# Seven-product blocks of a two-layer decoder trunk: the next block's weight split in eleven pieces, and another place for the sums of results

## The chip, the cores and the metric

The kernel runs on one core of one Trainium2 chip. The metric is the device time of one execution in microseconds (us). Engines are named as the profile names them: PE (TensorE, matmuls; PEld its weight loads), DVE (VectorE), ACT (ScalarE), POOL (GpSimd), SP (SyncE, which here only issues loads).

## The reference

The input is x, 512 tokens of 1024 channels, float32. Two layers of three sub-layers each, and a final norm:

```
for layer in (0, 1):
    x = x + 0.5 * swiglu(rmsnorm(x), w_gate, w_up, w_down)     # ffn1, inner width 2752
    x = x + mixer(rmsnorm(x))                                  # layer 0: S5 and attention; layer 1: short convolution
    x = x + 0.5 * swiglu(rmsnorm(x), w_gate, w_up, w_down)     # ffn2
out = rmsnorm(x)

def swiglu(h, w_gate, w_up, w_down):
    return (silu(h @ w_gate) * (h @ w_up)) @ w_down
```

The change touches the swiglu of layer 0's ffn2 and layer 1's ffn1 (n = 1 and n = 2 in the kernel, `SEVEN`).

## The kernel before, in words

**Precision.** Each float32 operand is split into a high part (a cast to a shorter float, on ACT, L214 for weights) and the rest (a subtraction on DVE, L220). A product of two operands is three matmuls: high by high, low by high, high by low. Weights arrive in a `raw` tile of 128 x 1024 (three of them), loaded by SP (L202); `refill` issues the load that reuses a raw tile once its last reader is done.

**Units.** A unit is one 128-row block of weights. `drive` runs a hand-written list of steps in order; every engine has one queue and works through it in that order. Ahead of a unit's matmuls `advance` splits the unit two places further on. The work of `ffn` comes in three thirds of the inner width. Each third first makes h (gate and up for its blocks f), then eight down units (dt = 0 to 7) that add to x, one per 128 channels. The down results use two PSUM banks (`ps_mm`), gate and up six (`ps_A`). After a down unit DVE adds the result to x (L539).

**Seven-product blocks.** For n = 1 and 2 the second and third third (seven blocks f each, 28 in all) are made with seven products of half size instead of eight (Winograd's form of Strassen's scheme). The weights of a block are the gate's halves A11, A12 and the up's halves A21, A22 along the channels; x is cut into halves B11, B12, B21, B22 along channels (first index) and tokens. With S1 = A21 + A22, S2 = S1 - A11, S3 = A11 - A21, S4 = A12 - S2 and T1 = B12 - B11, T2 = B22 - T1, T3 = B22 - B12, T4 = B21 - T2, one block issues on PE, all from line L667, 12 matmuls of 256 columns per product:

| | bank | product | what then reads the bank |
|---|---|---|---|
| 1 | x | A11 B11 | p1 = copy of x, ACT L687 |
| 2 | y | S2 T2 | u1 = y + p1, DVE L692 |
| 3 | x (added) | A12 B21 | silu, ACT L695: left half of the gate |
| 4 | y (added) | S1 T1 | u3 = y + p1, DVE L699 |
| 5 | z | S3 T3 | up_r = z + u3, DVE L703 |
| 6 | y (added) | S4 B22 | s_r = y + p1, DVE L706, then silu, ACT L707 |
| 7 | z (added) | A22 T4 | up_l = z + u1, DVE L709 |

After it h = s * up (DVE L710), its high part (ACT L713) and its low part (DVE L715). The low part is left in `pending` and runs in the next block or in `flush`. A product that adds to a bank must wait until the bank's reader is done: the third for p1, the fourth for u1, the sixth for u3, the seventh for up_r.

**The split of the next block** is handed out between the products by `more()`, which takes the next step of the generator `cuts`: first the gate's cast and subtraction (L214, L220), then `cut_mate` in four steps: cast of A22 (L262) with S1 (L263); S2 (L265) with the cast of S1, S2 (L266); S3 (L268), S4 (L269) and their cast (L270); the low part of A22 (L272) with two refills; then the two low parts of S (L278). `more()` is called right after a product's matmuls, ahead of the reader of its bank: after product 1 the gate's split stands ahead of p1, after product 2 the cast of A22 and S1 ahead of u1.

**Parts of x.** T1 to T4 and the parts of B are made once per ffn for four channel pairs i, in steps between the down units of the first third: `seven_sums(i)` (four DVE sums L627 to L632, four ACT casts L628 to L634) and `seven_lower(i)` (four DVE subtractions L642 to L646). `seven_parts(dt)` says which run after unit dt: sums 0 after dt 0, sums 1 and lower 0 after dt 1, lower 1 after dt 2, sums 2 after dt 3, lower 2 after dt 4, sums 3 after dt 5, lower 3 after dt 6. The split of the first seven-product block stands ahead of dt 6 and 7.

**The tail.** The inner width 2752 is 21 blocks of 128 and one of 64 + 64 (`TAIL`), whose h is made by a longer chain (L504 to L514). For n = 1 and 2 it is a unit of the first third, after f = 1; there the norm's factors become known, and two blocks' sums run late.

Of the kernel before, what the change touches and what calls it, by code (L numbers as in the profile page):

```python
# [8 lines left out]
F32 = mybir.dt.float32  # L9
# [3 lines left out]
ALU = mybir.AluOpType  # L13
# [8 lines left out]
TAIL = 21  # L22
# [121 lines left out]
class Trunk:  # L144
# [101 lines left out]

    def cut_mate(self, n):

        nc, sp = self.nc, self.sp7
        v = nc.vector
        u = self.units[n]
        g, w = u.mate.raw, u.raw
        a, b = slice(0, 512), slice(512, 1024)
        u.q_hi = sp.tile([128, 512], F32R, tag="ahi", name="ahi", bufs=2)
        u.q_lo = sp.tile([128, 512], F32R, tag="alo", name="alo", bufs=2)
        s = [sp.tile([128, 1024], F32, tag="s12", name="s12"), sp.tile([128, 1024], F32, tag="s34", name="s34")]
        u.s_hi = [sp.tile([128, 1024], F32R, tag="shi", name="shi", bufs=3) for _ in range(2)]  # L260
        u.s_lo = [sp.tile([128, 1024], F32R, tag="slo", name="slo", bufs=3) for _ in range(2)]
        nc.scalar.copy(u.q_hi, w[:, b])  # L262
        v.tensor_tensor(s[0][:, a], w[:, a], w[:, b], ALU.add)  # L263
        yield
        v.tensor_tensor(s[0][:, b], s[0][:, a], g[:, a], ALU.subtract)  # L265
        nc.scalar.copy(u.s_hi[0], s[0])  # L266
        yield
        v.tensor_tensor(s[1][:, a], g[:, a], w[:, a], ALU.subtract)  # L268
        v.tensor_tensor(s[1][:, b], g[:, b], s[0][:, b], ALU.subtract)  # L269
        nc.scalar.copy(u.s_hi[1], s[1])  # L270
        yield
        v.tensor_tensor(u.q_lo, w[:, b], u.q_hi.bitcast(F32), ALU.subtract)  # L272
        self.split = n + 1
        self.refill(n - 1)
        self.refill(n)
        yield
        for i in range(2):
            v.tensor_tensor(u.s_lo[i], s[i], u.s_hi[i].bitcast(F32), ALU.subtract)  # L278
            yield

    def drive(self):

# [175 lines left out]
    def ffn(self, n, nxt):  # L458
# [4 lines left out]
        nc = self.nc  # L463

        thirds = THIRDS[n]
# [82 lines left out]
        for third in range(3):  # L548
            seven = n in SEVEN and third
            if seven:  # L550
                pairs = [(Unit(gu[n, 2 * f], 1024, None, None), Unit(gu[n, 2 * f + 1], 1024, None, None)) for f in thirds[third]]
                for f, (g, u) in zip(thirds[third], pairs):
                    g.paired, u.mate = True, g
                    st.steps += [[g, u], lambda f=f, u=u: st.seven_products(f, u)]
                st.steps.append(st.flush)
            for f in [] if seven else sorted(thirds[third], key=lambda f: (f != TAIL or third == 0, f if f != TAIL else 1.5)):
                keep = []
                if f == TAIL:
                    st.steps.append(Unit(gu[n, 2 * f], 1024, st.over_x("A", keep), evac_tail(keep)))
                    continue  # L560
                g, u = evac_gate(keep, f), evac_up(keep, f)
                if f == 0:
                    early, keep0 = [g, u], keep
                    g = u = None
                    if n == st.first_ffn:
                        g, u = (lambda r=r: [st.feed_sq(st.first_norm, k) for k in r] for r in (range(4), range(4, 8)))
                elif f == 1:
                    def ug(g=g, u=u, keep=keep):
                        st.norm_bcast()
                        for kp, (gg, uu) in ((keep0, early), (keep, (g, u))):  # L570
                            pu = kp.pop()
                            gg()
                            kp.append(pu)
                            uu()
                    g, u = st.norm_sums, ug
                pair = [Unit(gu[n, 2 * f], 1024, st.over_x("A", keep), g), Unit(gu[n, 2 * f + 1], 1024, st.over_x("A", keep), u)]
                if f == 0 and n == st.first_ffn:
                    pair[0].products = lambda u, p=pair, k=keep: st.over_x_two("A", p, [k, k])
                    pair[1].products = lambda u: None
                st.steps += pair  # L580
                if n in SEVEN and 3 <= f < 7:
                    st.steps.append(lambda i=f - 3: st.seven_x(n, i))
            if third == 2 and nxt == 6:
                st.steps.insert(-1, st.advance)
                st.steps.append(st.advance)
                st.last_down([down(dt, third) for dt in range(NK)])
                break
            for dt in range(NK):
                s = down(dt, third)
                more = n in SEVEN and third < 2  # L590
                if more and dt == 6:
                    st.steps.append(st.advance)
                s.split_before = more and dt == 7
                st.steps.append(s)
                if more and third == 0:
                    st.steps += [lambda p=p: p() for p in st.seven_parts(dt)]
# [14 lines left out]

    def seven_parts(self, dt):

        i = {0: 0, 1: 1, 3: 2, 5: 3}.get(dt)
        j = {1: 0, 2: 1, 4: 2, 6: 3}.get(dt)
        return [lambda: self.seven_sums(i)] * (i is not None) + [lambda: self.seven_lower(j)] * (j is not None)

    def seven_sums(self, i):

# [27 lines left out]
        self.t7[i], self.b7[i] = (hi, lo), (b, o)  # L647

    def flush(self):
        if self.pending is not None:  # L650
            self.pending()
        self.pending = None

    def seven_products(self, f, u):

        nc, v, g = self.nc, self.nc.vector, u.mate
        cut = self.cuts(2)
        more = lambda: next(cut, None)
        l, r = slice(0, 256), slice(256, 512)

        def product(ps, w, c, b, first):

            for k in range(4):
                hi, lo = (p[:, c + k * 128:c + k * 128 + 128] for p in w)
                xhi, xlo = b(k)
                for n, (a, m) in enumerate(((hi, xhi), (lo, xhi), (hi, xlo))):
                    nc.tensor.matmul(  # L667
                        ps, a, m, start=first and k == 0 and n == 0, stop=k == 3 and n == 2, skip_group_check=True)

        def part(j):  # L670
            return lambda k: [p[:, j * 256:j * 256 + 256] for p in self.b7[k]]

        def total(j):
            c = slice(j % 2 * 256, j % 2 * 256 + 256)
            return lambda k: [p[j // 2][:, c] for p in self.t7[k]]

        b11, b21, b22 = (part(j) for j in range(3))
        t1, t2, t3, t4 = (total(j) for j in range(4))
        gate, s12, s34 = (g.hi, g.lo), (u.s_hi[0], u.s_lo[0]), (u.s_hi[1], u.s_lo[1])
        s = self.fp.tile([128, S], F32, tag="s", name="s", bufs=2)  # L680
        up = self.fp.tile([128, S], F32, tag="t", name="up", bufs=2)
        p1, u3 = up[:, l], s[:, r]
        u1 = self.tp.tile([128, S], F32, tag="sq", name="u1", bufs=2)[:, l]
        x = self.bank("A")[:, l]
        product(x, gate, 0, b11, True)
        more()
        nc.scalar.copy(p1, x)  # L687
        self.flush()
        y = self.bank("A")[:, l]
        product(y, s12, 512, t2, True)  # L690
        more()
        v.tensor_tensor(u1, y, p1, ALU.add)  # L692
        product(x, gate, 512, b21, False)
        more()
        nc.scalar.activation(s[:, l], x, AF.Silu)  # L695
        more()
        product(y, s12, 0, t1, False)
        more()
        v.tensor_tensor(u3, y, p1, ALU.add)  # L699
        z = self.bank("A")[:, l]  # L700
        product(z, s34, 0, t3, True)
        more()
        v.tensor_tensor(up[:, r], z, u3, ALU.add)  # L703
        product(y, s34, 512, b22, False)
        more()
        v.tensor_tensor(s[:, r], y, p1, ALU.add)  # L706
        nc.scalar.activation(s[:, r], s[:, r], AF.Silu)  # L707
        product(z, (u.q_hi, u.q_lo), 0, t4, False)
        v.tensor_tensor(up[:, l], z, u1, ALU.add)  # L709
        v.tensor_tensor(s, s, up, ALU.mult)  # L710
        hi = self.fp.tile([128, S], F32R, tag="hhi", name="hhi", bufs=8)
        lo = self.fp.tile([128, S], F32R, tag="hlo", name="hlo", bufs=8)
        nc.scalar.copy(hi, s)  # L713
        self.h[f] = (hi, lo)
        self.pending = lambda: v.tensor_tensor(lo, s, hi.bitcast(F32), ALU.subtract)  # L715
        deque(cut, maxlen=0)

    def last_down(self, units):
# [1218 lines left out]
```

## Time and profile before

| | |
|---|---|
| median of 3 runs (lowest to highest) | 1884.87 us (1883.11 to 1886.81) |
| profiled execution, its own time | 1882.82 us |
| its span, first to last instruction | 1881.1 us |
| busy in the span: PE, DVE, ACT, POOL | 97%, 64%, 37%, 6% |
| granted TensorE clock, mean | 0.996 of full speed |

The span is what the profile divides into shares; the rest of the profiled time lies around it. A busy PE is not a PE at its peak, since matmuls overlap and their ends are modelled: from one matmul's start to the next is the pace. In timeline rows the first number is the start in us from the span's start, the second the duration; [a <-b] is the engine's idle time before it and what ended it.

### The profile page before, as it was taken

The page shows a single profiled execution, that of the slowest core. Times are in us where ns is not written, and L with a number is a line of the kernel's source. Part 1 is how long each engine was busy: PE and PEld are TensorE (multiplying, and loading weights), DVE is VectorE, ACT ScalarE, POOL GpSimd, SP SyncE. Part 2 cuts the span into 40 slices and gives each one's busy share as a digit, 9 for nine tenths or more (in the row PEclk, how much of TensorE's full clock was granted, in tenths as well). Part 3 has the DMA queues.
Part 4 walks back from the last instruction along what each step waited for, and adds up shares of the span by engine and source line. Part 5 has one row for each costly group of instructions (what it writes and reads, how often), then busy time and mean ns, then how long its engine had stood idle before and what let it go on. Part 6 is the DMA issues. An engine that isn't in the chain of part 4 may idle for free.

```text
span 1881.1 us, 24317 instructions
## 1 busy us (share of the span) xinstructions
PE 1828.1 (97%) x9494; PEld 1558.1 (83%) x9494; DVE 1204.3 (64%) x1941; ACT 697.9 (37%) x1037; POOL 115.5 (6%) x238
## 2 busy tenths in 40 slices
PE   9999999999989999999999999999999999999998
PEld 8878888888867788888888888888888888888888
DVE  6757778656886568848756688576655545344444
ACT  5322322444885334424343344243322333222233
POOL 0280000100002000000010000000200110000000
PEclk9999999999989999999999999999999999999999
DMA  4334444456312232232232322322323223323331
GB/s 168 108 96 146 127 143 126 136 188 221 100 34 73 85 98 99 89 102 90 83 108 90 101 90 87 104 90 83 101 98 101 92 87 112 96 95 90 101 103 65
DMA packets 80146, 197.88 MB, mean 105 GB/s; under 512 B 20560, under 2 KB 29792, under 8 KB 80032
## 3 DMA queue, kind: packets, MB, share of 16 engines
q1 hardware_dynamic: 79856, 196.30, 32.5%
q8 instruction: 74, 1.21, 0.3%
q14 instruction: 40, 0.33, 0.1%
q10 hardware_dynamic: 144, 0.03, 0.0%
q0 software_dynamic: 32, 0.01, 0.0%
HBM read 180.45 MB, written 12.58 MB: 103 GB/s over the span
## 4 chain that ended last, share of the span: by engine, by line
PE 80%; DVE 8%; ACT 5%; issue 3%; POOL 3%; DMA 0%; DVEq 0%; SPq 0%; POOLq 0%; ACTq 0%
PE ps_A L302 13%; PE ps_A L301 13%; PE ps_A L303 13%; PE ps_A L667 10%; PE ps_mm L301 7%; PE ps_mm L302 7%; PE ps_mm L303 7%; ACT whi L214 2%; DVE wlo L220 1%; DVE s L710 1%; DVE hlo L715 1%; ACT hhi L713 1%; DVE s L263 1%; PE ps_mm L1640 1%; PE ps_A L1235 1%
## 5 line engine op out<-in xcount | busy, mean ns | idle before, releaser
L220 DVE TENSOR_TENSOR wlo<-raw,whi 128x1024 fp32r<-128x1024 f32 (+1 forms) x296 | 363.9, 1230 | 164.5 <-ACT whi L214 163.6
L302 PE MATMUL ps_A<-xhi,wlo 128*128 128x512 f32 x1120 | 436.4, 390 | 3.0 <-DVE wlo L220 2.9
L301 PE MATMUL ps_A<-xhi,whi 128*128 128x512 f32 x1120 | 437.6, 391 | 0.1
L303 PE MATMUL ps_A<-xlo,whi 128*128 128x512 f32 x1120 | 436.0, 389 | 0.1
L214 ACT CAST whi<-raw 128x1024 fp32r<-128x1024 f32 (+1 forms) x296 | 302.5, 1023 | 304.7 <-PE ps_mm L303 156.4
L301 PE MATMUL ps_mm<-hhi,whi 128*128 128x512 f32 (+1 forms) x672 | 256.7, 382 | 0.0
L302 PE MATMUL ps_mm<-hhi,wlo 128*128 128x512 f32 (+1 forms) x672 | 256.4, 382 | 0.0
L303 PE MATMUL ps_mm<-hlo,whi 128*128 128x512 f32 (+1 forms) x672 | 256.3, 381 | 0.0
L302 PEld LDWEIGHTS ps_A<-xhi,wlo 128*128 128x128 f32 x1120 | 210.3, 188 | 47.8 <-DVE wlo L220 4.4
L301 PEld LDWEIGHTS ps_A<-xhi,whi 128*128 128x128 f32 x1120 | 210.2, 188 | 45.4 <-ACT whi L214 0.9
L303 PEld LDWEIGHTS ps_A<-xlo,whi 128*128 128x128 f32 x1120 | 210.2, 188 | 44.3 <-DVE xlo L359 0.5
L301 PEld LDWEIGHTS ps_mm<-hhi,whi 128*128 128x128 f32 x672 | 126.3, 188 | 24.6 <-issue 0.4
L303 PEld LDWEIGHTS ps_mm<-hlo,whi 128*128 128x128 f32 x672 | 126.3, 188 | 24.4
L302 PEld LDWEIGHTS ps_mm<-hhi,wlo 128*128 128x128 f32 x672 | 126.3, 188 | 24.1
L539 DVE SCALAR_TENSOR_TENSOR x<-ps_mm,x 128x512 f32<-128x512 f32 x88 | 60.7, 690 | 108.1 <-PE ps_mm L303 100.7
L667 PE MATMUL ps_A<-thi,shi 128*128 128x256 f32 x336 | 97.7, 291 | 21.3 <-DVE u L692 21.3
L483 ACT ACTIVATE s<-t 128x512 f32<-128x512 f32 x56 | 35.4, 632 | 181.4 <-DVE t L481 181.4
L494 ACT CAST hhi<-s 128x512 fp32r<-128x512 f32 x56 | 34.8, 621 | 180.4 <-DVE s L493 180.4
L667 PE MATMUL ps_A<-thi,slo 128*128 128x256 f32 x336 | 95.0, 283 | 0.0
L667 PE MATMUL ps_A<-tlo,shi 128*128 128x256 f32 x336 | 95.0, 283 | 0.0
L667 PEld LDWEIGHTS ps_A<-thi,shi 128*128 128x128 f32 x336 | 64.3, 191 | 26.6 <-DVE u L692 26.6
L349 POOL TENSOR_TENSOR acc<-acc,sq 128x512 f32<-128x512 f32 x28 | 36.3, 1295 | 798.1 <-ACT sq L342 798.1
(404 smaller groups left out, 2940.6 us busy)
## 6 DMA issues: line engine op xcount, KB each, us to landing
raw<-gu SPq DMA_DIRECT2D x170, 512.0 KB, 3.4
raw<-dn SPq DMA_DIRECT2D x80, 448.0 KB, 3.3
raw<-sci SPq DMA_DIRECT2D x24, 512.0 KB, 3.4
raw<-dn SPq DMA_DIRECT2D x16, 512.0 KB, 3.5
raw<-ab SPq DMA_DIRECT2D x16, 512.0 KB, 3.5
raw<-abo SPq DMA_DIRECT2D x8, 512.0 KB, 3.5
raw<-sco SPq DMA_DIRECT2D x8, 512.0 KB, 3.4
x<-xT SPq DMA_DIRECT2D x8, 256.0 KB, 5.2
```

The source lines that it names most:

```text
L214: self.nc.scalar.copy(u.hi[:, : u.cols], u.raw[:, : u.cols])
L220: (engine or self.nc.vector).tensor_tensor(u.lo[:, :c], u.raw[:, :c], u.hi[:, :c].bitcast(F32), ALU.subtract)
L263: v.tensor_tensor(s[0][:, a], w[:, a], w[:, b], ALU.add)
L301: nc.tensor.matmul(ps, whi, xhi, start=start and i == 0, stop=False)
L302: nc.tensor.matmul(ps, wlo, xhi, start=False, stop=False)
L303: nc.tensor.matmul(ps, whi, xlo, start=False, stop=stop and i == n - 1)
L349: e.tensor_tensor(self.acc, self.acc, sq, ALU.add)
L483: nc.scalar.activation(s, t, AF.Silu)
L494: nc.scalar.copy(hi, s)
L539: nc.vector.scalar_tensor_tensor(x, keep[0], 0.5, x, ALU.mult, ALU.add)
L667: nc.tensor.matmul(ps, a, m, start=first and k == 0 and n == 0, stop=k == 3 and n == 2, skip_group_check=True)
L710: v.tensor_tensor(s, s, up, ALU.mult)
```

## The change

`cut_mate` becomes `mate_pieces`, which returns eleven named pieces; the last low part (of S3, S4) is cut in two. In a block whose follower is a seven-product block, `more(names)` issues pieces by name, and each reader of a bank stands right after the product that ends it, ahead of the pieces. After product 7 nothing is issued: up_l, the product with up, h's high part and its low part become a list in `pending`; the first three run after the next block's first product, ahead of p1, the low part behind the first pieces. `flush` runs all four at the end of a third. Where the follower is a down unit, its split is issued at two fixed places. `seven_parts` is: sums 0 and 1 after dt 0; lower 0, sums 2 after dt 1; lower 1, sums 3 after dt 2; lower 2 after dt 3; lower 3 after dt 4. The tail's unit moves from after f = 1 to after f = 4 (the sort key 1.5 becomes 4.5).

```diff
--- before.py
+++ after.py
@@ -246,6 +246,13 @@
     def cut_mate(self, n):
+        p = self.mate_pieces(n)
+        for i in ("a_hi", "s1", "s2", "s12_hi", "s3", "s4", "s34_hi", "a_lo", "s12_lo", "s34_lo0", "s34_lo1"):
+            p[i]()
+        yield
+    def mate_pieces(self, n):
@@ -259,24 +266,29 @@
         s = [sp.tile([128, 1024], F32, tag="s12", name="s12"), sp.tile([128, 1024], F32, tag="s34", name="s34")]
         u.s_hi = [sp.tile([128, 1024], F32R, tag="shi", name="shi", bufs=3) for _ in range(2)]
         u.s_lo = [sp.tile([128, 1024], F32R, tag="slo", name="slo", bufs=3) for _ in range(2)]
-        nc.scalar.copy(u.q_hi, w[:, b])
-        v.tensor_tensor(s[0][:, a], w[:, a], w[:, b], ALU.add)
-        yield
-        v.tensor_tensor(s[0][:, b], s[0][:, a], g[:, a], ALU.subtract)
-        nc.scalar.copy(u.s_hi[0], s[0])
-        yield
-        v.tensor_tensor(s[1][:, a], g[:, a], w[:, a], ALU.subtract)
-        v.tensor_tensor(s[1][:, b], g[:, b], s[0][:, b], ALU.subtract)
-        nc.scalar.copy(u.s_hi[1], s[1])
-        yield
-        v.tensor_tensor(u.q_lo, w[:, b], u.q_hi.bitcast(F32), ALU.subtract)
-        self.split = n + 1
-        self.refill(n - 1)
-        self.refill(n)
-        yield
-        for i in range(2):
-            v.tensor_tensor(u.s_lo[i], s[i], u.s_hi[i].bitcast(F32), ALU.subtract)
-            yield
+        def lower(i, c=slice(0, 1024)):
+            v.tensor_tensor(u.s_lo[i][:, c], s[i][:, c], u.s_hi[i][:, c].bitcast(F32), ALU.subtract)
+        def a_lo():
+            v.tensor_tensor(u.q_lo, w[:, b], u.q_hi.bitcast(F32), ALU.subtract)
+            self.split = n + 1
+            self.refill(n - 1)
+            self.refill(n)
+        return {
+            "a_hi": lambda: nc.scalar.copy(u.q_hi, w[:, b]),
+            "s1": lambda: v.tensor_tensor(s[0][:, a], w[:, a], w[:, b], ALU.add),
+            "s2": lambda: v.tensor_tensor(s[0][:, b], s[0][:, a], g[:, a], ALU.subtract),
+            "s12_hi": lambda: nc.scalar.copy(u.s_hi[0], s[0]),
+            "s3": lambda: v.tensor_tensor(s[1][:, a], g[:, a], w[:, a], ALU.subtract),
+            "s4": lambda: v.tensor_tensor(s[1][:, b], g[:, b], s[0][:, b], ALU.subtract),
+            "s34_hi": lambda: nc.scalar.copy(u.s_hi[1], s[1]),
+            "a_lo": a_lo,
+            "s12_lo": lambda: lower(0),
+            "s34_lo0": lambda: lower(1, a),
+            "s34_lo1": lambda: lower(1, b),
+        }
     def drive(self):
@@ -553,7 +565,7 @@
                     g.paired, u.mate = True, g
                     st.steps += [[g, u], lambda f=f, u=u: st.seven_products(f, u)]
                 st.steps.append(st.flush)
-            for f in [] if seven else sorted(thirds[third], key=lambda f: (f != TAIL or third == 0, f if f != TAIL else 1.5)):
+            for f in [] if seven else sorted(thirds[third], key=lambda f: (f != TAIL or third == 0, f if f != TAIL else 4.5)):
                 keep = []
                 if f == TAIL:
                     st.steps.append(Unit(gu[n, 2 * f], 1024, st.over_x("A", keep), evac_tail(keep)))
@@ -611,9 +623,8 @@
     def seven_parts(self, dt):
-        i = {0: 0, 1: 1, 3: 2, 5: 3}.get(dt)
-        j = {1: 0, 2: 1, 4: 2, 6: 3}.get(dt)
-        return [lambda: self.seven_sums(i)] * (i is not None) + [lambda: self.seven_lower(j)] * (j is not None)
+        return [lambda: self.seven_lower(dt - 1)] * (1 <= dt <= 4) + [
+            lambda i=i: self.seven_sums(i) for i in {0: (0, 1), 1: (2,), 2: (3,)}.get(dt, ())]
     def seven_sums(self, i):
@@ -647,15 +658,23 @@
         self.t7[i], self.b7[i] = (hi, lo), (b, o)
     def flush(self):
-        if self.pending is not None:
-            self.pending()
+        for p in self.pending or ():
+            p()
         self.pending = None
     def seven_products(self, f, u):
         nc, v, g = self.nc, self.nc.vector, u.mate
-        cut = self.cuts(2)
-        more = lambda: next(cut, None)
+        n = self.split
+        more = lambda *names: None
+        if n < len(self.units) and self.units[n].paired:
+            mate = self.mate_pieces(n + 1)
+            mate["hi"] = lambda: self.cut_hi(n)
+            mate["lo"] = lambda: self.cut_lo(n)
+            more = lambda *names: [mate[i]() for i in names]
+            cut = iter(())
+        else:
+            cut = self.cuts(2)
         l, r = slice(0, 256), slice(256, 512)
         def product(ps, w, c, b, first):
@@ -683,36 +702,43 @@
         u1 = self.tp.tile([128, S], F32, tag="sq", name="u1", bufs=2)[:, l]
         x = self.bank("A")[:, l]
         product(x, gate, 0, b11, True)
-        more()
+        late, self.pending = self.pending or [], None
+        for p in late[:3]:
+            p()
         nc.scalar.copy(p1, x)
-        self.flush()
+        more("s1", "s3", "hi")
+        for p in late[3:]:
+            p()
         y = self.bank("A")[:, l]
         product(y, s12, 512, t2, True)
-        more()
         v.tensor_tensor(u1, y, p1, ALU.add)
+        more("a_hi", "lo")
+        next(cut, None)
         product(x, gate, 512, b21, False)
-        more()
         nc.scalar.activation(s[:, l], x, AF.Silu)
-        more()
+        more("s2", "s12_hi", "s4", "s34_hi")
         product(y, s12, 0, t1, False)
-        more()
         v.tensor_tensor(u3, y, p1, ALU.add)
+        more("s12_lo")
+        next(cut, None)
         z = self.bank("A")[:, l]
         product(z, s34, 0, t3, True)
-        more()
         v.tensor_tensor(up[:, r], z, u3, ALU.add)
+        more("a_lo", "s34_lo0")
         product(y, s34, 512, b22, False)
-        more()
         v.tensor_tensor(s[:, r], y, p1, ALU.add)
+        more("s34_lo1")
         nc.scalar.activation(s[:, r], s[:, r], AF.Silu)
         product(z, (u.q_hi, u.q_lo), 0, t4, False)
-        v.tensor_tensor(up[:, l], z, u1, ALU.add)
-        v.tensor_tensor(s, s, up, ALU.mult)
         hi = self.fp.tile([128, S], F32R, tag="hhi", name="hhi", bufs=8)
         lo = self.fp.tile([128, S], F32R, tag="hlo", name="hlo", bufs=8)
-        nc.scalar.copy(hi, s)
         self.h[f] = (hi, lo)
-        self.pending = lambda: v.tensor_tensor(lo, s, hi.bitcast(F32), ALU.subtract)
+        self.pending = [
+            lambda: v.tensor_tensor(up[:, l], z, u1, ALU.add),
+            lambda: v.tensor_tensor(s, s, up, ALU.mult),
+            lambda: nc.scalar.copy(hi, s),
+            lambda: v.tensor_tensor(lo, s, hi.bitcast(F32), ALU.subtract),
+        ]
         deque(cut, maxlen=0)
     def last_down(self, units):
```

## Rows read from the trace of the kernel before

**Rows 1.** The page: its first line, and the chain that ended last, by engine.

```profile
span 1881.1 us, 24317 instructions
...
PE 80%; DVE 8%; ACT 5%; issue 3%; POOL 3%; DMA 0%; DVEq 0%; SPq 0%; POOLq 0%; ACTq 0%
```

**Rows 2.** Line L667: what PE's idle time ended with; us, times.

```profile
  DVE u L692: 47.8, 50
  ACT up L687: 18.7, 48
```

**Rows 3.** Timeline of PE: first matmuls of blocks, and two waits inside one.

```profile
734.42 0.28 PE L667 MATMUL ps_A<-bhi,whi 128*128 128x256 f32 x1
...
746.45 0.28 PE L667 MATMUL ps_A<-bhi,whi 128*128 128x256 f32 x1
...
749.80 0.38 PE L667 MATMUL ps_A<-bhi,whi 128*128 128x256 f32 x1 [0.31 <-ACT up L687]
...
752.33 0.39 PE L667 MATMUL ps_A<-thi,shi 128*128 128x256 f32 x1 [0.84 <-DVE u L692]
...
805.10 0.28 PE L667 MATMUL ps_A<-bhi,whi 128*128 128x256 f32 x1
...
817.00 0.40 PE L301 MATMUL ps_mm<-hhi,whi 128*128 128x512 f32 x1
...
855.11 0.28 PE L667 MATMUL ps_A<-bhi,whi 128*128 128x256 f32 x1
...
865.18 0.28 PE L667 MATMUL ps_A<-bhi,whi 128*128 128x256 f32 x1
```

**Rows 4.** Timeline of DVE, the block that starts at 746.45.

```profile
746.65 0.42 DVE L709 TENSOR_TENSOR up<-ps_A,u 128x256 f32<-128x256 f32 x1 [0.44 <-PE ps_A L667]
747.18 0.69 DVE L710 TENSOR_TENSOR s<-s,up 128x512 f32<-128x512 f32 x1
749.51 1.22 DVE L220 TENSOR_TENSOR wlo<-raw,whi 128x1024 fp32r<-128x1024 f32 x1 [1.63 <-ACT whi L214]
750.65 0.69 DVE L715 TENSOR_TENSOR hlo<-s,hhi 128x512 fp32r<-128x512 f32 x1
...
751.85 0.42 DVE L692 TENSOR_TENSOR u<-ps_A,up 128x256 f32<-128x256 f32 x1
752.19 0.68 DVE L265 TENSOR_TENSOR s<-s,raw 128x512 f32<-128x512 f32 x1
```

**Rows 5.** Timeline of ACT, the same block.

```profile
747.91 0.62 ACT L713 CAST hhi<-s 128x512 fp32r<-128x512 f32 x1 [1.24 <-DVE s L710]
748.43 1.04 ACT L214 CAST whi<-raw 128x1024 fp32r<-128x1024 f32 x1
749.38 0.36 ACT L687 COPY up<-ps_A 128x256 f32<-128x256 f32 x1
```

**Rows 6.** Loads of raw tiles in 734 to 936 us, from issue to landing.

```profile
DMA to landing us min/median/max: 3.2/3.6/5.1
```

**Rows 7.** Timelines of PE and DVE, down units of the first third.

```profile
697.92 0.39 PE L301 MATMUL ps_mm<-hhi,whi 128*128 128x512 f32 x1
...
713.57 0.39 PE L301 MATMUL ps_mm<-hhi,whi 128*128 128x512 f32 x1
...
737.33 0.39 PE L667 MATMUL ps_A<-blo,whi 128*128 128x256 f32 x1 [1.44 <-DVE blo L645]
...
698.73 0.42 DVE L627 TENSOR_TENSOR t<-xn 128x256 f32<-128x256 f32 x1
...
702.44 1.23 DVE L220 TENSOR_TENSOR wlo<-raw,whi 128x1024 fp32r<-128x1024 f32 x1 [2.16 <-ACT whi L214]
...
705.64 1.29 DVE L642 TENSOR_TENSOR tlo<-t,thi 128x512 fp32r<-128x512 f32 x2
...
707.89 1.23 DVE L220 TENSOR_TENSOR wlo<-raw,whi 128x1024 fp32r<-128x1024 f32 x1
```

**Rows 8.** Timeline of PE, the third unit after the tail.

```profile
649.28 0.50 PE L302 MATMUL ps_A<-xhi,wlo 128*128 128x512 f32 x1 [0.77 <-DVE wlo L220]
```

## The prediction, made before the changed kernel ran

> **What bounds the kernel now.** The page comes first. The span is 1881.1 us, and 80% of the chain of work that ended last lies on TensorE (PE) [rows 1]. So a gain here must be time in which PE waits. Next I read the view of the one line that issues all matmuls of the seven-product blocks, L667, and look at what ended PE's idle time before it: 50 waits for the sum u1 (VectorE, DVE, L692) and 48 for the copy p1 (ScalarE, ACT, L687) [rows 2]. A place shows up to twice, once at the weight load and once at the matmul, so they are some 24 of each, nearly one per block. Then I read PE's timeline at the first matmul of each block. A block of 84 matmuls in which nothing waits takes 865.18 - 855.11 = 10.07 us. The usual block takes (805.10 - 746.45) / 5 = 11.73 [rows 3]. Inside it PE stops at 749.80 for the copy p1, ahead of the third product, and at 752.33 for u1, ahead of the fourth [rows 3].
>
> Why are these late? With the block's start (746.45) as zero, p1 starts at 2.93, although the first product ended at 1.44 (10.07 / 7): on ACT it stands behind the 1024-wide cast of the next gate weights, which starts at 1.98 [rows 5]. The sum u1 starts at 5.40, although the second product ended at 2.88: on DVE it stands behind wlo, hlo and s1, and wlo had to wait 1.63 for that cast [rows 4]. So each block loses 1.66 us to order in two queues, not to lack of engine time.
>
> **The change part by part.**
>
> *Prices.* Start to start, DVE takes 0.34 for 256 columns (751.85 to 752.19), 0.60 for 512 (two of them, hlo and s1, from 750.65 to 751.85) and 1.14 for 1024 (749.51 to 750.65) [rows 4]. ACT takes 0.52 for 512 (747.91 to 748.43) and 0.95 for 1024 (748.43 to 749.38) [rows 5]. A result of a product is read 0.20 after the next product starts (746.45 to 746.65) [rows 3, 4]. A product takes 1.44, so products 3, 4, 6 and 7 are due at 2.88, 4.32, 7.19 and 8.63.
>
> *The usual block in the new order.* DVE: up_l at 0.20, s*up 0.73 (0.53 later, as now), s1 1.33, s3 1.93, lo 2.53, u1 3.13 to 3.55. PE needs u1 at 4.32: 0.7 to spare. ACT: hi at 1.46 (as now, 747.91), p1 at 1.98 to 2.35, due 2.88: 0.5 to spare. Behind them cut_hi runs from 2.24, cut_lo 3.47, s2 4.61, s4 5.3, u3 5.95 to 6.37 (due 7.19). The cast s12_hi waits for s2 and ends at 6.4; s12_lo starts there; up_r 7.55 to 7.97 (due 8.63, the narrowest of DVE's, 0.66). Then a_lo 7.9, s34_lo0 8.5, s_r 9.1, s34_lo1 9.4 to 10.0, and the next up_l may start at 10.27. No product waits, so the block falls to 10.07. Every weight is there a product or more before use.
>
> *Does DVE have room?* Per block it has five operations of 256, nine of 512 and two of 1024: 1.70 + 5.40 + 2.28 = 9.38, plus 0.19 for s*up behind up_l (0.53 instead of 0.34) and 0.1, an estimate from the same pair, for s4 behind s2: 9.7 of 10.07. The split of s34_lo into two adds 2 x 0.60 - 1.14 = 0.06, inside that. The cover is thin, but it holds. Here a rule speaks against the change. The rows show DVE starting an operation 1.14 after one that lasts 1.22 (749.51 and 750.65), so neighbours overlap by 0.08 [rows 4]. The Trainium skill (VectorE: DVE Perf Modes, The DRAIN you can't avoid) says that after each operation the next waits until the pipe is empty, and adds that one which nothing holds starts earlier. By its first half DVE's block would be the sum of full durations, and PE would follow DVE: the second rival below. The rows side with the second half.
>
> *Gain of the blocks.* There are 28. Twenty lose 11.73 - 10.07 = 1.66: 33.2 us. The last block of each third (four) takes 817.00 - 805.10 = 11.90 and loses 1.83: 7.3. The first after the first third (two) takes 746.45 - 734.42 = 12.03 [rows 3]; most of its loss is the wait for blo (1.44 idle, [rows 7]); with blo made earlier it loses nothing: 3.9. The other two, as at 855.11, wait for nothing already. Sum 44.4.
>
> *Ends of a third.* up_l, s*up, hi and lo of the last block now come in the flush: 0.20 + 0.42 + 0.1 + 0.69 + 0.62 + 0.68, about 2.8 us after the last product. The first down projection reads that h in its 19th matmul, 18 x 0.227 = 4.1 later, so the price is nothing; without that cover it would be 2.8 four times.
>
> *SP's queue.* SP issues only loads here. The refill of the gate's buffer waits for s4, which now ends at 6.0; the other waits for a_lo, ending at 8.6. The first must land before s1 of the next block at 11.4: 5.3 us, against 3.2 to 5.1 measured [rows 6]. Price nothing, bounds 0 and, at 5.1 plus some contention, 0.3 per block.
>
> *The parts of x between the down projections.* This one costs. A down unit takes PE (713.57 - 697.92) / 3 = 5.22 [rows 7]. One set of sums holds DVE from 698.73 to the next split at 702.44, 3.71 us, because ACT casts the sums first and the split's own cast is queued behind. A seven_lower takes 707.89 - 705.64 = 2.25 at most [rows 7]. After down units 1 and 2 DVE now has a lower and a set of sums: 0.60 for x, 2.2, 3.71, 1.14 for the split: 7.6, against PE's 5.22. Followed from unit 0 (two sets, second set's casts behind the first's: split at 703.9 to 704.3): x of unit 1 starts at 705.0 to 705.4, x of unit 2 at 712.6 to 713.0, x of unit 3 at 720.2 to 720.6. There are two banks for these results, so unit 4 (713.57) must wait for x of unit 2, which ends at 713.3 to 713.7, and unit 5 (then 718.8 to 719.1) for x of unit 3, ending at 720.9 to 721.3. Loss 1.8 to 2.8; I take 2.7 for the later ends, because the casts of eight sums stand on ACT by then. Twice (two layers' third): +5.4, bounds 0 and 6.
>
> *The tail's place.* At 649.28 PE waits for a split that stood behind the tail's chain on DVE and ACT: 0.77 idle [rows 8], 0.2 of overlap lost and a slow restart, some 1.2. It occurs twice. Behind f = 4 DVE is no longer catching up: -2.4, bounds 0 and 3.
>
> **Sum.** -44.4 + 5.4 - 2.4 = -41.4. The profiled execution took 1882.82 (its span and 1.7 around it): 1841.4. The median shown is 2.05 above that execution, so on its scale I say 1843.5.
>
> **The rivals.** (1) No wait between the down projections: x comes in time. Against: the 7.6 against 5.22. It gives 1843.5 - 5.4 = 1838.1. (2) DVE becomes the bound. By full durations [rows 4], 5 x 0.42 + 9 x 0.68 + 2 x 1.22 = 10.66 a block, 0.6 over PE, in 24 blocks: +14.4, 1857.9. Against: the overlap just named. (3) The change does only half of what it says, because p1 still waits on ACT behind hi, and hi behind two DVE operations. If u1 came 0.8 after the fourth product was due, about half of today's loss, the sum would be 0.8 x 24 = 19.2 worse: 1862.7. Against: hi stands at 1.46 today with the same two operations ahead of it [rows 5]. (4) Slower than before: the refill loop. s1 of the next block now heads DVE's queue and waits for a load which s4 releases; from s1 to the end of s4 are 4.7 us. With a landing of L the block takes 4.75 + L. It decides from L = 5.3, and costs more than now from L = 7.0. At 7.5 the block is 12.25: 24 x 0.52 = 12.5 worse, with the rest -0.9, 1896.5. Against: 3.2 to 5.1 us [rows 6].
>
> **How the numbers follow.** Forecast 0.68, with its own range 1839 to 1848; rival 1 0.14; rival 2 0.12; rival 3 0.04; rival 4 0.02. The range 1836 to 1853 takes the forecast, rival 1 and the lesser half of rival 2's cost. About 0.2% (3.8 us) can be told from no change. All but rival 4 are faster by far more: faster 0.97, same 0.01, slower 0.02.
>
> **What would show it.** Right: first matmuls of blocks 10.1 apart; the two waits of rows 2 gone; DVE's u1 near 3.1 of the block; wlo behind the tail no longer waited for; and a new PE wait for x (L539) before the fifth and sixth down units of a first third. Wrong: DVE without gaps and blocks of 10.5 or more; idle on DVE ahead of s1 until a load lands; or no PE wait between the down projections.

## The result, and the profile after

| | before | after |
|---|---|---|
| median (lowest to highest), 4 runs each | 1884.32 us (1883.11 to 1886.81) | 1843.18 us (1842.37 to 1846.27) |
| profiled execution, its own time | 1882.82 us | 1846.27 us |
| its span | 1881.1 us | 1844.6 us |
| busy in the span: PE, DVE | 97%, 64% | 99%, 66% |

The ratio of after to before is 0.9783, with a 95% interval from 0.9766 to 0.98: faster by 41.1 us in the medians. The forecast was 1843.5 us, 41.4 less.

The page of after: its first line, and the chain that ended last, by engine. They answer to [rows 1].

```profile
span 1844.6 us, 24331 instructions
...
PE 88%; DVE 4%; POOL 3%; ACT 3%; issue 1%; DMA 0%; SPq 0%; DVEq 0%; POOLq 0%; ACTq 0%
```

PE's share of the chain grew from 80% to 88%, and those of DVE and ACT fell from 8% and 5% to 4% and 3%. What left the chain is the waits of the seven-product blocks. Their line is L686 in after. Its view, which in [rows 2] named u1 and p1 as what ended PE's idle time, now has nothing between these two lines:

```profile
its engine sat idle before it (us, times) until:
who waited for it (us, times):
```

PE's timeline of after, the first matmuls of blocks and of the down unit that follows the last of a third; these answer to [rows 3].

```profile
740.50 0.28 PE L686 MATMUL ps_A<-bhi,whi 128*128 128x256 f32 x1
...
750.58 0.28 PE L686 MATMUL ps_A<-bhi,whi 128*128 128x256 f32 x1
...
800.98 0.28 PE L686 MATMUL ps_A<-bhi,whi 128*128 128x256 f32 x1
...
811.06 0.40 PE L313 MATMUL ps_mm<-hhi,whi 128*128 128x512 f32 x1
```

The first block after a first third, the five between 750.58 and 800.98 and the last of the third all take 10.08 us. All 28 blocks stand at 10.07 or 10.08, the time of 84 matmuls among which nothing waits. Before, the first took 12.03, the five 11.73 each and the last 11.90 [rows 3].

DVE's timeline of after in the block whose first product starts at 770.74 (750.58 and two blocks); it answers to [rows 4].

```profile
770.94 0.42 DVE L737 TENSOR_TENSOR up<-ps_A,u 128x256 f32<-128x256 f32 x1 [0.16 <-PE ps_A L686]
771.47 0.69 DVE L738 TENSOR_TENSOR s<-s,up 128x512 f32<-128x512 f32 x1
772.08 0.69 DVE L281 TENSOR_TENSOR s<-raw 128x512 f32<-128x512 f32 x1
772.68 0.69 DVE L284 TENSOR_TENSOR s<-raw 128x512 f32<-128x512 f32 x1
...
773.89 0.42 DVE L714 TENSOR_TENSOR u<-ps_A,up 128x256 f32<-128x256 f32 x1
774.23 1.22 DVE L220 TENSOR_TENSOR wlo<-raw,whi 128x1024 fp32r<-128x1024 f32 x1
...
778.31 0.42 DVE L726 TENSOR_TENSOR up<-ps_A,s 128x256 f32<-128x256 f32 x1
```

With the block's start as zero, u1 (L714) starts at 3.15 instead of 5.40, and up_r (L726) at 7.57. The gate's wlo (L220) stands behind u1 and no longer ahead of it. DVE's one idle stretch of the block is the 0.16 ahead of up_l. ACT's timeline of the same block answers to [rows 5].

```profile
772.20 0.62 ACT L739 CAST hhi<-s 128x512 fp32r<-128x512 f32 x1 [1.56 <-DVE s L738]
772.72 0.36 ACT L708 COPY up<-ps_A 128x256 f32<-128x256 f32 x1
772.98 1.05 ACT L214 CAST whi<-raw 128x1024 fp32r<-128x1024 f32 x1
```

The copy p1 (L708) starts at 1.98 of the block instead of 2.93: the 1024-wide cast now stands behind it.

The new wait lies in the down units of a first third, as the prediction placed it. PE's timeline of after, at the first matmuls of the fifth and the sixth unit (the [..] gives PE's idle time); it answers to [rows 7].

```profile
716.63 0.39 PE L547 MATMUL ps_mm<-hi,wlo 128*128 128x512 f32 x1
717.18 0.47 PE L313 MATMUL ps_mm<-hhi,whi 128*128 128x512 f32 x1 [0.16 <-DVE x L551]
...
722.25 0.39 PE L547 MATMUL ps_mm<-hi,wlo 128*128 128x512 f32 x1
724.76 0.47 PE L313 MATMUL ps_mm<-hhi,whi 128*128 128x512 f32 x1 [2.12 <-ACT whi L214]
```

The usual step from one matmul to the next is 0.227. Here it is 0.55 and 2.51, so these two units come 0.32 and 2.28 late, and each loses another 0.08 in a slow restart, since the step after it takes 0.31: 2.76. The view names whi for the second wait, but that cast had ended at 722.8. DVE's timeline of after tells which it was:

```profile
716.35 0.68 DVE L551 SCALAR_TENSOR_TENSOR x<-ps_mm,x 128x512 f32<-128x512 f32 x1
...
722.79 1.23 DVE L220 TENSOR_TENSOR wlo<-raw,whi 128x1024 fp32r<-128x1024 f32 x1 [2.15 <-ACT whi L214]
723.93 0.68 DVE L551 SCALAR_TENSOR_TENSOR x<-ps_mm,x 128x512 f32<-128x512 f32 x1
```

The second x (L551), which frees the bank of two units before, ends at 724.61, and PE starts 0.15 later. It stands behind a split that had waited 2.15 for its cast, and comes 7.58 after the x before it; PE needs 5.22 for a unit [rows 7]. A wait for several semaphores is written down under one name; where that one had long been done, look for another that ended just before.

The profiled execution of after is 3.1 us above its median. The trace puts this ahead of the first instruction that the change touches, in layer 0's mixer. PE's timelines show it at two rows of matmuls there that both kernels have (x2 and x16 are rows of two and of sixteen matmuls). Before:

```profile
437.18 0.41 PE L1380 MATMUL ps_mm<-sh,tab_ca 128*128 128x63 f32 x2
...
450.17 1.89 PE L1331 MATMUL ps_mm<-u,tab_wv 128*128 128x64 f32 x16
```

After:

```profile
438.69 0.41 PE L1406 MATMUL ps_mm<-sh,tab_ca 128*128 128x63 f32 x2 [1.20 <-DVE ut L1336]
...
454.88 1.89 PE L1357 MATMUL ps_mm<-u,tab_wv 128*128 128x64 f32 x16
```

After is 1.51 behind at the first row, most of it the wait of 1.20, and 4.71 behind at the second. Between the two lies a stretch at a lower clock. It shows in the two kernels' windows; the columns are the stretch and its length in us, busy time (count) of PE, PEld, DVE, ACT and POOL, the granted clock, DMA share and GB/s. After:

```profile
441.00:448.00 7.00, 7.00 (x24) 6.05 (x24) 0.70 (x1) 1.63 (x2) 0.00 (x0) 0.54 0.62 202
```

Before:

```profile
441.00:448.00 7.00, 7.00 (x32) 5.75 (x32) 1.23 (x1) 1.38 (x2) 0.00 (x0) 1.00 0.69 216
```

From 441 to 448 us PE ran at 0.54 of full speed, so mostly at the 1.2 GHz level, and got through 24 matmuls instead of 32. That stretch costs 4.71 - 1.51 = 3.2. The whole delay from ahead of the change is the shift of the first changed block, 740.50 - 734.42 [rows 3] = 6.08, of which 2.76 are the new waits just read and -1.44 the tail (below): 4.8 are left. Measured from before's trace, the profiled execution would have taken about 1841.5 without these 4.8, and the sum of the prediction was 1841.4 on that scale.

### The profile page after: what moved, and what is told of

Read it like the earlier page. It is cut to its first block, busy times and chain, and to the rows that moved or that the text cites. A ratio compares the mean times of both kernels' runs of the same rounds, so it can differ in the third digit from the quotient of the medians.

```text
span 1844.6 us, 24331 instructions
## 1 busy us (share of the span) xinstructions
PE 1818.7 (99%) x9494; PEld 1559.1 (85%) x9494; DVE 1210.6 (66%) x1969; ACT 699.0 (38%) x1037; POOL 115.5 (6%) x238
## 4 chain that ended last, share of the span: by engine, by line
PE 88%; DVE 4%; POOL 3%; ACT 3%; issue 1%; DMA 0%; SPq 0%; DVEq 0%; POOLq 0%; ACTq 0%
PE ps_A L686 15%; PE ps_A L313 14%; PE ps_A L315 14%; PE ps_A L314 14%; PE ps_mm L313 7%; PE ps_mm L314 7%; PE ps_mm L315 7%; DVE wlo L220 1%; ACT whi L214 1%; PE ps_mm L1666 1%; PE ps_A L1261 1%; PE ps_mm L1668 1%; PE ps_mm L1667 1%; PE ps_A L1263 1%; PE ps_A L1262 1%
## 5 line engine op out<-in xcount | busy, mean ns | idle before, releaser
L220 DVE TENSOR_TENSOR wlo<-raw,whi 128x1024 fp32r<-128x1024 f32 (+1 forms) x296 | 364.5, 1232 | 131.3 <-ACT whi L214 130.5
L551 DVE SCALAR_TENSOR_TENSOR x<-ps_mm,x 128x512 f32<-128x512 f32 x88 | 60.7, 690 | 105.9 <-PE ps_mm L315 99.9
L686 PE MATMUL ps_A<-thi,shi 128*128 128x256 f32 x336 | 95.1, 283 | 0.0
L686 PE MATMUL ps_A<-thi,slo 128*128 128x256 f32 x336 | 95.1, 283 | 0.0
L686 PE MATMUL ps_A<-tlo,shi 128*128 128x256 f32 x336 | 95.1, 283 | 0.0
L365 ACT ACTIVATE xhi<-x,norms 128x512 fp32r<-128x512 f32 x48 | 34.5, 723 | 101.4 <-DVE x L551 63.4
```

The costliest lines, as they stand in the source:

```text
L220: (engine or self.nc.vector).tensor_tensor(u.lo[:, :c], u.raw[:, :c], u.hi[:, :c].bitcast(F32), ALU.subtract)
L365: self.nc.scalar.activation(hi, self.x[k], AF.Copy, scale=self.norms[:, which, k:k + 1])
L551: nc.vector.scalar_tensor_tensor(x, keep[0], 0.5, x, ALU.mult, ALU.add)
L686: nc.tensor.matmul(ps, a, m, start=first and k == 0 and n == 0, stop=k == 3 and n == 2, skip_group_check=True)
```

## The experiments

Eight kernels, each timed beside the kernel before, whose median was 1884.64 us in the runs with e1 to e4 and 1884.11 us with e5 to e8. They do the same arithmetic, but for e6, which writes half of one low part twice. Single executions of one kernel scatter by 2 to 7 us, so where two versions lie closer than that the trace's own waits decide.

### e1: the old order of the parts of x

```diff
     def seven_parts(self, dt):
-        return [lambda: self.seven_lower(dt - 1)] * (1 <= dt <= 4) + [
-            lambda i=i: self.seven_sums(i) for i in {0: (0, 1), 1: (2,), 2: (3,)}.get(dt, ())]
+        i = {0: 0, 1: 1, 3: 2, 5: 3}.get(dt)
+        j = {1: 0, 2: 1, 4: 2, 6: 3}.get(dt)
+        return [lambda: self.seven_sums(i)] * (i is not None) + [lambda: self.seven_lower(j)] * (j is not None)
```

> The changed kernel with the parts of x in their old places between the down units. Theory (the parts' new places make PE wait for x before the fifth and sixth down unit of each first third, 2.7 us twice, and take away the first block's wait for blo): the two waits before those down units go (-5.4 us), a wait for blo of 1.4 us idle, 1.7 in all, comes back in the first block, twice (+3.4). Together 2.0 us faster than the changed kernel: 1841.2. Rival (the old places were worse on the whole, as the change implies): 3.4 to 4 us slower than the changed kernel, about 1847, with no wait that goes away.

Measured: 1841.13 us (1839.73 to 1842.03), ratio 0.9769 [0.9756, 0.9782], 2.05 below after. The intervals overlap; the trace of e1 shows what happened. Both waits before the down units are gone, and the wait for blo in the first block after a first third is back. PE's timeline of e1:

```profile
738.50 0.39 PE L687 MATMUL ps_A<-blo,whi 128*128 128x256 f32 x1 [1.51 <-DVE blo L657]
```

With the slow restart that wait costs 1.77, in two places 3.5, against the 5.5 that go: 2.0 in e1's favour. So the new order of the parts, taken alone, loses more between the down units than it gains in the first block. The 5.5 is real, which speaks against rival 1, by which x would have come in time.

### e2: sums and lower parts of one pair after each of the first four down units

```diff
     def seven_parts(self, dt):
-        return [lambda: self.seven_lower(dt - 1)] * (1 <= dt <= 4) + [
-            lambda i=i: self.seven_sums(i) for i in {0: (0, 1), 1: (2,), 2: (3,)}.get(dt, ())]
+        return [lambda: self.seven_sums(dt), lambda: self.seven_lower(dt)] * (dt < 4)
```

> The changed kernel with sums i and lower i both behind down unit i (i = 0 to 3). Theory: while ACT casts the sums, DVE does the lower instead of standing idle for 2.2 us ahead of the next split, so a unit costs DVE about 0.6 + 1.5 + 2.2 + 1.1 = 5.4 and some waits, little over PE's 5.22, and x is never late for a bank: both PE waits before down units go (-5.4) and blo is still early. 1837.8, and the first block starts 2.7 us earlier in the stage. Rival (the same eight parts on the same four units load DVE as much, so the wait stays): within 1 us of the changed kernel, 1842 to 1844.

Measured: 1837.16 us (1836.51 to 1839.34), ratio 0.9749 [0.9736, 0.9762]. It is 6.0 below after, beyond both intervals, and the best of all versions run. DVE's timeline of e2 from the x of one down unit to that of the next:

```profile
705.58 0.68 DVE L551 SCALAR_TENSOR_TENSOR x<-ps_mm,x 128x512 f32<-128x512 f32 x1
...
707.75 1.36 DVE L652 TENSOR_TENSOR tlo<-t,thi 128x512 fp32r<-128x512 f32 x2
...
711.10 0.68 DVE L551 SCALAR_TENSOR_TENSOR x<-ps_mm,x 128x512 f32<-128x512 f32 x1
```

Such a unit holds DVE for 5.52 us (705.58 to 711.10) with as much work as the 7.6 of after, since the low parts run while ACT does the casts and the split's cast is ready when its turn comes; DVE is not idle. (After's 7.6 is read above: 7.58 from x to x, with the 2.15 of waiting in it.) That is 0.3 over PE's 5.22 a unit, and two banks of results bridge it for four units: PE waits at none. In after the order of the queue within a unit, not the amount of work there, made x late. e2 also takes the second set of sums out of the first unit; how much of the 6.0 that gives by itself was not tried. blo is early enough as well.

### e3: the tail's old place

```diff
-            for f in [] if seven else sorted(thirds[third], key=lambda f: (f != TAIL or third == 0, f if f != TAIL else 4.5)):
+            for f in [] if seven else sorted(thirds[third], key=lambda f: (f != TAIL or third == 0, f if f != TAIL else 1.5)):
```

> The changed kernel with the tail's unit again behind f = 1. Theory: the wait for the weight split in the third unit behind the tail comes back, 0.77 idle and about 1.2 to 1.4 us in all, twice: 2.4 to 2.7 us slower than the changed kernel, 1845.7. Rival (the place of the tail is off the path): within 0.5 us, no PE wait on a weight split of over 0.5 us in the first third.

Measured: 1847.66 us (1842.69 to 1848.12), ratio 0.9798 [0.9783, 0.9813]. Its median is 4.5 above after, but the ranges overlap, and its profiled execution has a stretch at a lower granted clock of its own (0.72 from 1068 to 1074 us), in which eight steps take about 0.42 instead of 0.23, 1.6 in all. It follows PE's wait of 2.08 before the sixth down unit of layer 1, one of the waits that the change brought; after has the same wait, and 1.00 over the same stretch. The tail's wait itself is read from PE's timeline of e3:

```profile
650.20 0.50 PE L313 MATMUL ps_A<-xhi,whi 128*128 128x512 f32 x1
651.46 0.50 PE L314 MATMUL ps_A<-xhi,wlo 128*128 128x512 f32 x1 [0.76 <-DVE wlo L220]
```

A step of 1.26 instead of 0.23, with the slow restart 1.44, and 1.20 at the second place: 2.6 in all, the wait of [rows 8]. In after none of it is left, and no other wait came in its place.

### e4: eleven pieces, but each ahead of the reader

```diff
-        nc.scalar.copy(p1, x)
         more("s1", "s3", "hi")
+        nc.scalar.copy(p1, x)
...
-        v.tensor_tensor(u1, y, p1, ALU.add)
         more("a_hi", "lo")
+        v.tensor_tensor(u1, y, p1, ALU.add)
```

The other four readers likewise.

> The changed kernel with the same eleven pieces, but each call that hands them out ahead of the reader of the bank instead of behind it. Theory (what counts is that the reader stands first in its queue): p1 stands behind the gate's cast again, u3 behind the low part of S1, S2; PE waits 0.6 ahead of the third product, 0.4 ahead of the sixth and 0.1 ahead of the seventh; a block takes 11.1 instead of 10.07, 24 times: +25 us, 1868. Rival (the finer grain of the split and the later end of the block make the gain): blocks of 10.1 to 10.3, 1843 to 1849.

Measured: 1863.24 us (1862.62 to 1864.71), ratio 0.9888 [0.9875, 0.9902]: 20.1 above after, about half of the gain. PE's timeline of e4:

```profile
758.38 0.28 PE L686 MATMUL ps_A<-bhi,whi 128*128 128x256 f32 x1
...
769.48 0.28 PE L686 MATMUL ps_A<-bhi,whi 128*128 128x256 f32 x1
```

and ACT's in the same block:

```profile
760.37 1.05 ACT L214 CAST whi<-raw 128x1024 fp32r<-128x1024 f32 x1
761.32 0.36 ACT L709 COPY up<-ps_A 128x256 f32<-128x256 f32 x1
```

The block takes 11.10, and p1 starts at 2.94 of it behind the 1024-wide cast, as in the kernel before. The sixth product starts late too (a step of 0.39 instead of 0.12), so u3 is late as expected. Twenty blocks at 1.02 more make 20.4; the expectation counted 24. The last block of each third hands out no pieces, and in the first, which hands them out, p1 is not held up: those eight stay at 10.08 and 10.07.

### e5: the kernel before, with each reader ahead of its `more()`

```diff
         product(x, gate, 0, b11, True)
-        more()
         nc.scalar.copy(p1, x)
+        more()
...
         product(y, s12, 512, t2, True)
-        more()
         v.tensor_tensor(u1, y, p1, ALU.add)
+        more()
```

The other readers likewise; nothing else of the change is in it.

> The kernel before, with each of its seven calls that hand out the split moved behind the reader of the bank, and nothing else. Theory (the reader's place alone does not do it: DVE still stands idle while ACT casts h's high part, copies p1 and then casts the next gate weights, and the gate's low part, h's low part and then u1 follow that): p1 is early, PE's wait ahead of the third product goes, but the wait ahead of the fourth grows from 1.1 to about 1.5; a usual block takes 11.6 instead of 11.73; 4 to 6 us faster than the kernel before, 1878 to 1881. Rival (the reader's place is the whole gain): blocks of 10.1 to 10.3, about 1845 to 1850.

Measured: 1880.09 us (1877.59 to 1881.55, 11 runs), ratio 0.9978 [0.9969, 0.9987]: 4.0 below before. PE's timeline of e5:

```profile
749.24 0.28 PE L667 MATMUL ps_A<-bhi,whi 128*128 128x256 f32 x1
...
754.97 0.39 PE L667 MATMUL ps_A<-thi,shi 128*128 128x256 f32 x1 [1.25 <-DVE u L691]
...
760.83 0.28 PE L667 MATMUL ps_A<-bhi,whi 128*128 128x256 f32 x1
```

and DVE's in the next block:

```profile
764.35 1.23 DVE L220 TENSOR_TENSOR wlo<-raw,whi 128x1024 fp32r<-128x1024 f32 x1 [1.91 <-ACT whi L214]
765.49 0.68 DVE L715 TENSOR_TENSOR hlo<-s,hhi 128x512 fp32r<-128x512 f32 x1
766.09 0.42 DVE L691 TENSOR_TENSOR u<-ps_A,up 128x256 f32<-128x256 f32 x1
```

The wait for p1 is gone, but that for u1 grew. wlo was handed out together with its cast after product 1; it holds DVE's queue for 1.91 until the cast is through, and u1 comes behind it, at 5.26 of the block (5.40 before). The block still takes 11.59.

Kernels before and after, e4 and e5 make a square of four:

| usual block, us | pieces ahead of the reader | reader ahead of the pieces |
|---|---|---|
| the old handing out | 11.73 | 11.59 |
| eleven pieces by name | 11.10 (e4) | 10.08 |

Place alone gives 0.14, pieces alone 0.63, both 1.65: 0.88 needs both. The lower row changes several things in a block at once: the order of the pieces, the gate's cast and its subtraction one product apart, the eleventh piece and the late end of the block. e7 and e8 below take out the last two and lose nothing by it; the first two were not told apart. The reader first only helps if nothing handed out earlier stops the queue ahead of it.

### e6: one more DVE operation of 512 columns per block

```diff
-        more("a_lo", "s34_lo0")
+        more("a_lo", "s34_lo0", "s34_lo0")
```

> The changed kernel with one more 512-column subtraction on DVE per block with pieces: the first half of the low part of S3, S4 is written twice with the same values. Theory (DVE takes 9.7 of a block's 10.07, start to start, and the next operation of 512 adds 0.60): the block becomes DVE's, 10.4, and PE waits about 0.4 ahead of the third product, since the chain up_l, product, high part, p1 starts late; 20 such blocks, +7 us, 1850. Rival (DVE is the bound already): +0.60 to 0.68 in each, +12 to 14, 1855 to 1857. Other rival (DVE has ample room): no change.

Measured: 1854.91 us (1853.12 to 1859.01), ratio 0.985 [0.9837, 0.9864]: 11.7 above after. PE's timeline of e6:

```profile
768.21 0.28 PE L686 MATMUL ps_A<-bhi,whi 128*128 128x256 f32 x1
...
778.75 0.28 PE L686 MATMUL ps_A<-bhi,whi 128*128 128x256 f32 x1
```

DVE's, with the repeated pair counted as one row (x2):

```profile
767.00 1.41 DVE L271 TENSOR_TENSOR slo<-s,shi 128x512 fp32r<-128x512 f32 x2
768.33 0.42 DVE L729 TENSOR_TENSOR s<-ps_A,up 128x256 f32<-128x256 f32 x1
```

The pair takes 1.33 from its start to that of the next operation, so the second costs 0.73: it writes the columns that its predecessor just wrote. The usual block rises from 10.08 to 10.54, by 0.46. So some 0.27 of the 0.73 was hidden and the rest came out in PE's time: DVE, without idle time here, sets the pace. This measures the room that after's DVE has left, 0.27 us a block. Had DVE been the bound already, the block would have grown by the whole 0.60 to 0.73; with ample room, by nothing. The median lies nearer to the rival's 1855 than to the expected 1850, but the four runs lie 5.9 apart, and the 28 blocks of the trace add up to only 9.9 more than after's.

### e7: ten pieces

```diff
+            "s34_lo": lambda: lower(1),
...
-        more("a_lo", "s34_lo0")
+        more("a_lo")
...
-        more("s34_lo1")
+        more("s34_lo")
```

> The changed kernel with the last low part in one operation of 1024 columns in the last piece's place, so ten pieces. Theory (DVE has 0.07 us less to do per block and still waits for the last product): blocks of 10.08, no change within 1 us, 1842 to 1844. Rival (one long operation there makes s_r, up_l or p1 late): PE waits of 0.1 to 0.5 per block, 2 to 10 us slower.

Measured: 1843.66 us (1842.88 to 1847.67), ratio 0.9794 [0.9781, 0.9808]. PE's timeline of e7, the first matmuls of two blocks:

```profile
758.05 0.28 PE L687 MATMUL ps_A<-bhi,whi 128*128 128x256 f32 x1
...
768.13 0.28 PE L687 MATMUL ps_A<-bhi,whi 128*128 128x256 f32 x1
```

10.08, as in after. Cutting the last low part in two is worth nothing here.

### e8: the end of a block issued in its own place

```diff
-        late, self.pending = self.pending or [], None
-        for p in late[:3]:
-            p()
         nc.scalar.copy(p1, x)
         more("s1", "s3", "hi")
-        for p in late[3:]:
+        for p in late:
             p()
...
         product(z, (u.q_hi, u.q_lo), 0, t4, False)
+        v.tensor_tensor(up[:, l], z, u1, ALU.add)
+        v.tensor_tensor(s, s, up, ALU.mult)
...
+        nc.scalar.copy(hi, s)
+        self.pending = [lambda: v.tensor_tensor(lo, s, hi.bitcast(F32), ALU.subtract)]
```

> The changed kernel with up_l, the product with up and h's high part issued right after the seventh product, as before, and the low part alone left for the next block. Theory (on DVE and ACT nothing stands between these and the next block's first pieces, so each queue has the same order as in the changed kernel): blocks of 10.08, no change within 1 us, 1842 to 1844. Rival (their move behind the next first product is part of the gain): blocks of 10.3 and more, 5 us or more slower.

Measured: 1845.42 us (1842.69 to 1847.54), ratio 0.9796 [0.9783, 0.9809]; its profiled execution has the same stretch at a low clock in the mixer as that of after. PE's timeline of e8:

```profile
759.80 0.28 PE L686 MATMUL ps_A<-bhi,whi 128*128 128x256 f32 x1
...
769.88 0.28 PE L686 MATMUL ps_A<-bhi,whi 128*128 128x256 f32 x1
```

Again 10.08. Moving up_l, the product with up and hi behind the next block's first product changes the order in the source, but in the queues of DVE and ACT they stand where they stood: between product 7 and the next p1 neither engine was given anything else.

## Why the prediction was right

The terms of the sum, each against what the trace of after (and e3 for the tail) shows:

| term | forecast | measured |
|---|---|---|
| 20 usual blocks, 4 last, 2 first | -33.2 - 7.3 - 3.9 = -44.4 | -33.0 - 7.3 - 3.9 = -44.2 |
| waits before the fifth and sixth down units | +2.7 twice: +5.4 | +2.76 and +2.71: +5.5 |
| the tail's place | -2.4 | -2.6 |
| sum | -41.4 | -41.3; medians -41.1 |

- **The bound.** The loss was order in two queues. e4 and e5 show that both halves of the edit are needed for it, as the reading of p1 on ACT [rows 5] and of u1 on DVE [rows 4] said: e5 moves p1 and leaves u1 late, and in e4 PE waits for p1 and u3 and no longer for u1.
- **The new order.** Followed by start-to-start times, p1 was put at 1.98, u1 at 3.13 and up_r at 7.55; they stand at 1.98, 3.15 and 7.57.
- **DVE's room (rival 2).** Forecast 9.7 of 10.07. After's blocks don't follow DVE's full durations, and e6 adds 0.73 to DVE and gets 0.46 on the block. Room left is then 0.27, a little less than the 0.37 of the sum. The Trainium skill (VectorE: DVE Perf Modes, The DRAIN you can't avoid) has the next operation wait until the pipe is empty, and adds that one which is not held starts earlier. The trace of after sides with the addition: s3 starts 0.60 after s1, which lasts 0.69.
- **Half only (rival 3).** Refuted: L686 has no idle time left. e4 lands near its 1862.7 by another way: p1 is late there too, but behind the 1024-wide cast and not behind hi, so the agreement is chance.
- **No wait between the down units (rival 1).** Refuted by the 2.76, and e2 shows what that rival's time would have needed: another order, not less work. It gave 1837.16, where the rival put 1838.1.
- **The refill loop (rival 4).** Refuted: s1 (L281) starts without idle time ahead of it. The loads of the raw tile show why. The issue, on SP's queue, of the load that brings what s1 of the next block reads, and the line on landing in the view of these loads from 740 to 910 us, as in [rows 6]:

```profile
766.76 0.33 SPq L202 DMA_DIRECT2D raw<-gu  x1
...
DMA to landing us min/median/max: 3.2/3.4/5.1
```

It is issued 6.1 us into the block that starts at 760.66, and s1 of the next starts at 772.08, 5.3 later; the slowest landing is 5.1.

- **The size of the new wait.** The prediction chose the later of two ends for x of the fourth unit, and that end came: the split behind the eight sums waited 2.56 for its cast and starts at 707.61, which is 704.3 on before's times (the first of the sums starts at 702.03 in after and at 698.73 before [rows 7]). Its lower bound of 1.8 was too low by its own times, since it leaves out the 0.3 that the fifth unit has lost by then: 2.1.
- **The parts that were costed at nothing** (ends of a third, the two refills, eleven pieces) left no wait on PE, and e7 and e8 show the same for two of them.
- What the prediction left out is the level of a single execution: it set the sum on the median's scale by +2.05, while after's profiled execution sat 4.8 higher than before's for reasons ahead of the change.

## What to carry to other kernels

Where PE waits inside a block of fixed work, write down for each in-order queue what stands between the result and its reader, with start-to-start times instead of durations: the operation that frees a PSUM bank goes first, and an operation that waits for another engine's cast is issued only behind it. Work moved out of one stage fills another stage's queue: follow each moved piece there as well, and interleave it so that one engine's cast runs under the other's subtraction (e2, worth 6.0 us more). If a queue's cover is thin, add one operation of known price to it and see how much comes out.

## What the runs showed of the hardware that was not expected

- **A stretch at half clock that comes and goes.** In the profiled executions of after and e8, TensorE's granted clock falls to 0.54 and 0.58 over 441 to 448 us, and in the other eight it stays at 1.00 there. PE had waited just before, 1.20 us in after and 0.85 in e8. But a wait of that length does not decide it: e1 waits 1.00 at the same place and e2 1.63, and both keep the full clock. PE's timeline of e1:

```profile
438.68 0.41 PE L1407 MATMUL ps_mm<-sh,tab_ca 128*128 128x63 f32 x2 [1.00 <-DMA tab_ca<-drca]
```

The cost was worked out above as 3.2 us. Why some executions of the same instructions keep the full clock stays open; it was not tried. In e3 such a stretch stands right behind one of the waits that the change itself brought in; whether the wait brought it on is not shown either.

- **Writing the same columns twice.** On DVE a subtraction of 512 columns that rewrites what its predecessor just wrote took 0.73 from start to start, where one that touches other data took 0.60 (e6). What holds it up was not tried.
